# Layer 0's prologue with its token loads between the modulation halves and its norms ahead of the last halves

## The chip, the cores and the metric

The kernel runs on one core of one Trainium2 chip. The metric is device time in microseconds (us), the median of several runs; lower is better. A profiled execution also gives the time of every instruction on TensorE (PE, with its weight loads listed as PEld), VectorE (DVE), ScalarE (ACT), GpSimd (POOL) and the DMA issues of SyncE (SP). In the profile an engine name with a q behind it (SPq, ACTq) is that engine's queue.

## The reference, cut to what matters

The program is a two-layer diffusion backbone over 1024 latent tokens and 256 context tokens, model width 1024, in float32. Each layer begins in the same way: a conditioning vector gives a shift, a scale and a gate (the modulation), the tokens are RMS-normalised, scaled and shifted, and the result h feeds every projection of the layer.

```python
def rms_norm(x, g):
    y = xf * lax.rsqrt(jnp.mean(xf * xf, axis=-1, keepdims=True) + EPS)
    return (y * g.astype(jnp.float32)).astype(x.dtype)

def modulation(cond, w, b):
    m = jax.nn.silu(cond) @ w + b          # 1024 -> 3 * 1024
    return jnp.split(m, 3, axis=-1)        # shift, scale, gate

for i in range(DEPTH):                     # DEPTH = 2
    sh_l, sc_l, g_l = modulation(c, mod_w[i], mod_b[i])
    sh_c, sc_c, g_c = modulation(c_ctx, mod_w[i], mod_b[i])
    h_lat = rms_norm(x_lat, norm_g[i]) * (1.0 + sc_l[:, None, :]) + sh_l[:, None, :]
    h_ctx = rms_norm(x_ctx, norm_g[i]) * (1.0 + sc_c) + sh_c
    ...                                    # attention (layer 0), convolution and attention (layer 1)
    x_lat = x_lat + g_l[:, None, :] * y_lat
```

## The kernel before, in words

Activations lie with the model width on the partitions: 8 slices (dk) of 128 by the tokens. The tokens are cut in three chunks: chunk 0 is the 256 context tokens, chunks 1 and 2 are 512 latent tokens each. Products are made in split precision: every operand is kept as a high part and a low remainder, and one product is three matmuls (lines 316 to 318: high by high, high by low, low by high). So every h must be made as a pair, the high part by ACT and the low part by POOL or DVE.

The prologue of layer 0 is driven by a string, `PLAN`, one letter for one step, traced in this order:

- `p` loads the small bias and gain vectors.
- `0`, `1`, `2` ask for a chunk of tokens (tiles `xr`): chunk 0 as two DMAs, chunk 1 as two, chunk 2 as eight. All are issued from SP. `after_mod(XA)` puts a load behind the DMAs of the last four modulation tiles traced.
- `m` is one modulation half, `mod_half`: 512 output columns of shift or scale. Four weight tiles (`mw`, two dk slices each) come from HBM in a ring over buffers that the attention needs later (`KA`, `KB`, `V`) and two of its own; for each tile PE multiplies with the conditioning (`pm`, line 176, 32 columns of the array each); ACT copies the sum (`mrow`, line 203), eight small matmuls turn it round (`trm`, line 181), DVE adds the bias (`modT`, line 185), and for scale halves multiplies with the norm's gain (`gs`, line 187). The four halves are shift 0, shift 1, scale 0, scale 1; scale half 0 gives `gs` for dk 0 to 3, scale half 1 for dk 4 to 7.
- `n` is the sum of squares of the next chunk, `norm_x`: eight squares on ACT (lines 678 and 681) and seven additions on DVE (line 682) into `acc`.
- `b` is that chunk's reciprocal root laid over all partitions, `norm_bc`: matmuls with ones (`trs`, line 251), a power on POOL (line 238), three small DVE instructions (lines 239 to 241), and matmuls that broadcast the result (`bc`, line 261) into a PSUM bank.
- `w` asks for the first projection weights (`wr`), which ACT and POOL split (`wh`, `wl`). Two raw buffers serve four loads, so the last two wait until the first two are split.
- `h` makes the chunk's pair, `make_h`: for each dk one DVE multiplication by `gs` and `bc` (line 306), the shift on ACT (line 309 or 312), and the split (lines 296, 299, 310).

Behind the prologue `proj_qkv` makes ten blocks of 128 tokens, 24 matmuls each (`pq`): two blocks from chunk 0, four from chunk 1, four from chunk 2. Further modulation halves (the gate of layer 0 and all six of layer 1) are fed in between by `mod_steps`, with the same line 176.

The traced order is a priority and not yet the order of issue: the framework's scheduler fixes each engine's queue ahead of time on a simulated timeline (`schedule_with_timeline_sim=True`), taking what it believes ready. On the chip each queue then runs in that fixed order. PSUM banks are taken by tag: `st` has two banks, `ov` and `tr` one each; `trs` and `trm` share `tr`, `bc` uses `st`. `p0`, the pool of the projections' tiles, is opened when `st0`, the pool of the first two chunks' `xr`, is closed.

Of the kernel before, what the change touches and what calls it, by code (L numbers as in the profile page):

```python
# [69 lines left out]
HV = 'gggvvvvg'  # L70
O1 = (6, 65, 41, 14)
TICK0, TICK1 = (1, 3)
PLAN = 'p0mmnbwmm1h2nbhnbh'
MWR = "ABxAVx"
XA = 4
ORDER = (2, 3, 0, 1)
# [11 lines left out]
def tile_kernel(ctx: ExitStack, tc: tile.TileContext, a, out):  # L88
# [14 lines left out]
    def bank(tag, name):  # L103
        if tag == "pp" and solo[0]:
            turn[0] += 1
            tag = ("pp", "mx")[turn[0] // 2 % 2]
        return ps.tile([P, 512], F32, tag=tag, name=name, bufs=BUFS[tag])
# [3 lines left out]
    def nm(s):  # L111
        uid[0] += 1
        return f"{s}_{uid[0]}"
# [50 lines left out]
    @contextmanager  # L164
    def after_mod(k):

        with ExitStack() as cx:
            for m in mm0[-k:]:
                cx.enter_context(tc.issue_after(m.ins))
            yield  # L170
# [24 lines left out]
    def mod_half(l, part, j):  # L195

        pb = bank("pp", nm("pm"))
        for d2 in range(4):
            w2 = mw_tile()
            mm0.append(SY.dma_start(w2, mod_src(l, part, j, 2 * d2, 2 * d2 + 2)))  # L200
            mod_part(pb, w2, (2 * d2, 2 * d2 + 1))
        row = a0.tile([P, 512], F32, tag="ost", name=nm("mrow"), bufs=2)
        SC.copy(row, pb)
        mod_out(bank("tr", nm("trm")), row, l, part, j)
# [29 lines left out]
    def newton_rsqrt(pool, v, n, tag):  # L234

        r = pool.tile([P, 16], F32, tag=tag + "r", name=nm("nr"), bufs=2)
        t = pool.tile([P, 16], F32, tag=tag + "t", name=nm("nt"), bufs=2)
        GP.tensor_tensor(r[:, :n], v, mhalf[:, :n], op=ALU.pow)
        VE.tensor_tensor(t[:, :n], r[:, :n], v, op=ALU.mult)
        VE.scalar_tensor_tensor(t[:, :n], t[:, :n], -0.5, r[:, :n], op0=ALU.mult, op1=ALU.mult)  # L240
        VE.scalar_tensor_tensor(r[:, :n], t[:, :n], 1.5, r[:, :n], op0=ALU.add, op1=ALU.mult)
        return r

    def rstd_steps(pool, accs, n, tag, inv=1.0, tr="tr"):


        nb = n // P
        tr = bank(tr, nm("trs"))
        for b in range(nb):
            for k, acc in enumerate(accs):  # L250
                PE.matmul(tr[:, 2 * b : 2 * b + 2], acc[:, b * P : (b + 1) * P], ones, start=(k == 0),
                          stop=(k == len(accs) - 1))
        v = pool.tile([P, 8], F32, tag="rbv", name=nm("rbv"), bufs=2)
        VE.tensor_scalar(v[:, :nb], tr[:, 0 : 2 * nb].rearrange("p (b two) -> p b two", two=2)[:, :, 0],
                         inv, EPS, op0=ALU.mult, op1=ALU.add)
        r = newton_rsqrt(pool, v[:, :nb], nb, "rb")
        yield
        yield
        bc = bank(tag, nm("bc"))
        for b in range(nb):  # L260
            PE.matmul(bc[:, b * P : (b + 1) * P], r[:, b : b + 1].broadcast_to([P, P]), ident, start=True, stop=True)
        return bc
# [9 lines left out]
    def run(gen):  # L272

        while True:
            try:
                next(gen)
            except StopIteration as e:
                return e.value


    def new_h(c):
        if c == 0:
            t = bigp.tile([P, 2, DK, 256], F32R, tag="big", name=nm("hc"))
            return (t[:, 0], t[:, 1])
        th = bigp.tile([P, DK, 512], F32R, tag="big", name=nm("hh"))
        tl = bigp.tile([P, DK, 512], F32R, tag="big", name=nm("hl"))
        return (th, tl)
# [13 lines left out]
    def make_h(l, c, xs, bc, h):  # L301

        cond = 1 if c == 0 else 0
        for dk in range(DK):
            x = xs(dk)
            VE.scalar_tensor_tensor(x, x, gs[l][:, dk, cond : cond + 1], bc, op0=ALU.mult, op1=ALU.mult)
            shift = modT[l][:, dk, cond : cond + 1]
            if HV[dk] == "v":
                SC.activation(h[0][:, dk, :], x, AF.Identity, bias=shift)
                VE.scalar_tensor_tensor(h[1][:, dk, :], x, shift, h[0][:, dk, :].bitcast(F32), op0=ALU.add, op1=ALU.subtract)  # L310
            else:
                SC.activation(x, x, AF.Identity, bias=shift)
                split(x, h[0][:, dk, :], h[1][:, dk, :])
# [332 lines left out]
    with ExitStack() as p0x:  # L646
# [3 lines left out]
        def load_w0(src, u):  # L650
            return load_w(w0p, a[src], u, 384, W0B, rb=WRB)

        with tc.tile_pool(name="st0", bufs=1, reuse_waits="tile") as st0:
            for c in range(3):
                h[c] = new_h(c)
            xraw = {}

            def load_x(c):
                t0, n = CHUNKS[c]
                if c == 2:  # L660
                    tags = ["ph"] * 4 + ["pl"] * 4
                    xraw[c] = [a0.tile([P, n], F32, tag=t, name=nm("xr2"), bufs=LOOK0 + 1) for t in tags]
                else:
                    t = st0.tile([P, DK, n], F32, tag=f"xr{c}", name=f"xr{c}")
                    xraw[c] = [t[:, dk, :] for dk in range(DK)]
                    for d in range(0, DK, 4):
                        SY.dma_start(t[:, d : d + 4, :],
                                     a["cT"][:, d : d + 4, :] if c == 0 else a["xT"][:, d : d + 4, 0:n])
                    return
                for dk in range(DK):  # L670
                    SY.dma_start(xraw[c][dk], a["xT"][:, dk, t0 - 256 : t0 - 256 + n])

            def norm_x(c):
                n = CHUNKS[c][1]
                acc = kvp.tile([P, 512], F32, tag="QH", name=nm("acc"), bufs=3)
                for dk in range(DK):
                    if dk == 0:
                        SC.activation(acc[:, :n], xraw[c][0], AF.Square)
                    else:
                        sq = kvp.tile([P, 512], F32, tag="QL", name=nm("sq"), bufs=3)  # L680
                        SC.activation(sq[:, :n], xraw[c][dk], AF.Square)
                        VE.tensor_tensor(acc[:, :n], acc[:, :n], sq[:, :n], op=ALU.add)
                return acc

            def norm_bc(c, acc):
                n = CHUNKS[c][1]
                return run(rstd_steps(st0, [acc], n, "st"))[:, :n]

            made = [0]
            accs, bcs, mh = [], [], [(0, 0), (0, 1), (1, 0), (1, 1)]  # L690
            mwp[0] = st0
            for ev in PLAN:
                if ev in "012":
                    with after_mod(XA):
                        load_x(int(ev))
                elif ev == "p":
                    SC.dma_start(modb, a["mod_b"])
                    SC.dma_start(normg, a["norm_g"])
                elif ev == "n":
                    accs.append(norm_x(len(accs)))  # L700
                elif ev == "w":
                    with after_mod(XA):
                        w0 = load_w0("ev_qkv", ORDER[0])
                elif ev == "m":
                    mod_half(0, *mh.pop(0))
                elif ev == "b":
                    bcs.append(norm_bc(len(bcs), accs[len(bcs)]))
                elif ev == "h":
                    make_h(0, made[0], lambda dk, c=made[0]: xraw[c][dk], bcs[made[0]], h[made[0]])
                    made[0] += 1  # L710

            mwp[0] = None
# [142 lines left out]
        for k in range(4):  # L855
            u = ORDER[k]
            n = NSTEP[u // 2] + (12 if k == 0 else 0)
# [698 lines left out]
```

## Time and profile before

| what | value |
|---|---|
| median of 3 runs | 1595.98 us (1594.56 to 1597.62) |
| profiled execution, its time | 1590.1 us |
| its span, first to last instruction | 1588.3 us |
| PE busy | 1477.4 us, 93% of the span |
| DVE, POOL, ACT busy | 1087.8, 791.0, 745.3 us |
| HBM read and written | 153.84 and 54.79 MB |

Busy times are sums over an engine's instructions; the profile's windows give the same for a stretch, with the granted clock of TensorE (1.00 is full) and the DMA rate. A timeline row gives start, duration, engine, line and tile, and in brackets how long the engine had been idle and for what.

### The profile page before, as it was taken

How to read it: one execution, taken by the hardware profiler on the slowest of the kernel's cores; microseconds unless marked ns; L12 is line 12 of the kernel's file. 1: busy time of each engine (PE TensorE's matmuls, PEld its weight loads, DVE VectorE, ACT ScalarE, POOL GpSimd, SP SyncE). 2: the span in 40 equal slices, each digit the busy share in tenths (PEclk: the TensorE clock that was granted, in tenths of full speed). 3: DMA queues.
4: the chain of work that ended last, by engine and by line, in shares of the span. 5: the costliest groups of instructions: out<-in, count | busy, mean ns of one | idle time of the engine just before them, and what ended most of it. 6: DMA issues, size and time to landing. Idle time of an engine off the chain costs nothing.

```text
span 1588.3 us, 21721 instructions
## 1 busy us (share of the span) xinstructions
PE 1477.4 (93%) x7084; PEld 1178.0 (74%) x7084; DVE 1087.8 (68%) x2283; ACT 745.3 (47%) x1418; POOL 791.0 (50%) x633
## 2 busy tenths in 40 slices
PE   6899999999999999999989879999998899899995
PEld 2785988886886778876866657888877778777775
DVE  2833576588599855566778857999566465778776
ACT  3722334443435555457555754433333454545563
POOL 3531352553445676557555755654431343344575
PEclk7899999998999999999999989999999899899997
DMA  9473324422312363212112032213546877988732
GB/s 366 157 238 121 110 84 152 137 76 90 110 50 82 99 210 101 64 57 65 30 38 80 7 101 60 80 54 101 190 160 198 234 222 215 273 243 239 224 101 106
DMA packets 159929, 211.38 MB, mean 133 GB/s; under 512 B 15356, under 2 KB 96456, under 8 KB 159816
## 3 DMA queue, kind: packets, MB, share of 16 engines
q1 hardware_dynamic: 153152, 198.42, 39.8%
q10 hardware_dynamic: 6664, 11.57, 2.2%
q8 instruction: 56, 0.92, 0.3%
q14 instruction: 57, 0.47, 0.1%
HBM read 153.84 MB, written 54.79 MB: 131 GB/s over the span
## 4 chain that ended last, share of the span: by engine, by line
PE 67%; DVE 16%; DMA 7%; issue 4%; ACT 2%; POOL 2%; SPq 0%; DVEq 0%; ACTq 0%; POOLq 0%
PE p L316 6%; PE p L317 6%; PE p L318 6%; PE ov L426 4%; PE ov L428 4%; PE ov L427 4%; PE st L463 4%; PE st L467 3%; PE po L316 3%; PE po L317 3%; PE po L318 3%; PE pq L316 3%; PE pq L317 3%; PE pq L318 3%; PE pg L318 2%
## 5 line engine op out<-in xcount | busy, mean ns | idle before, releaser
L299 POOL TENSOR_TENSOR pl<-pf,ph 128x512 fp32r<-128x512 f32 (+4 forms) x321 | 393.8, 1238 | 361.5 <-ACT ph L296 289.4
L299 POOL TENSOR_TENSOR wl<-wr,wh 128x512 fp32r<-128x512 f32 (+2 forms) x131 | 170.6, 1314 | 181.1 <-ACT wh L296 150.6
L475 ACT ACTIVATE pf<-st 128x512 f32<-128x512 f32 x284 | 165.6, 596 | 200.7 <-PE st L467 153.0
L296 ACT CAST ph<-pf 128x512 fp32r<-128x512 f32 (+4 forms) x364 | 209.6, 588 | 27.9 <-PE ov L427 17.7
L316 PE MATMUL p<-hh,wh 128*128 128x512 f32 x448 | 180.1, 402 | 8.6 <-ACT hh L296 2.8
L317 PE MATMUL p<-hl,wh 128*128 128x512 f32 x448 | 178.7, 400 | 0.9 <-POOL hl L299 0.9
L318 PE MATMUL p<-hh,wl 128*128 128x512 f32 x448 | 176.4, 400 | 0.0
L463 PE MATMUL st<-QH,KAt 128*128 128x512 f32 (+4 forms) x364 | 142.6, 393 | 10.0 <-ACT pf L475 8.1
L426 PE MATMUL ov<-ph,Vt 128*128 128x512 f32 (+4 forms) x364 | 141.3, 388 | 7.8 <-DVE y L625 6.2
L428 PE MATMUL ov<-pl,Vt 128*128 128x512 f32 (+4 forms) x364 | 141.6, 389 | 1.6 <-POOL pl L299 0.9
L427 PE MATMUL ov<-ph,Vt 128*64 128x512 f32 (+4 forms) x364 | 139.8, 384 | 0.0
L467 PE MATMUL st<-QL,KBt 68*128 68x512 f32 (+4 forms) x364 | 136.6, 388 | 0.0
L1041 DVE SCALAR_TENSOR_TENSOR cps<-U,taps,cps 128x512 f32<-128x512 f32 x184 | 126.4, 751 | 0.9
L296 ACT CAST wh<-wr 128x512 fp32r<-128x512 f32 (+2 forms) x134 | 81.1, 613 | 88.8 <-PE p L317 19.9
L316 PEld LDWEIGHTS p<-hh,wh 128*128 128x128 f32 x448 | 85.5, 191 | 31.3 <-ACT hh L296 3.0
L588 DVE TENSOR_REDUCE mp<-mx 128x1 f32<-128x512 f32 x128 | 85.9, 683 | 28.1 <-PE mx L587 27.5
L317 PEld LDWEIGHTS p<-hl,wh 128*128 128x128 f32 x448 | 85.1, 190 | 21.8 <-POOL hl L299 1.9
L318 PEld LDWEIGHTS p<-hh,wl 128*128 128x128 f32 x448 | 85.1, 190 | 19.9
L316 PE MATMUL pq<-wh,hh 128*128 128x384 f32 x256 | 88.4, 345 | 2.8 <-ACT hh L296 2.8
L463 PEld LDWEIGHTS st<-QH,KAt 128*128 128x128 f32 x364 | 70.1, 193 | 28.1 <-ACT pf L475 12.1
L426 PEld LDWEIGHTS ov<-ph,Vt 128*128 128x128 f32 x364 | 70.5, 194 | 23.9 <-issue 6.9
L428 PEld LDWEIGHTS ov<-pl,Vt 128*128 128x128 f32 x364 | 70.2, 193 | 24.1 <-POOL pl L299 5.0
(274 smaller groups left out, 3508.4 us busy)
## 6 DMA issues: line engine op xcount, KB each, us to landing
mw<-in_mod_w_dram SPq DMA_DIRECT2D x16, 1024.0 KB, 6.1
Q<-qs SPq DMA_DIRECT2D x40, 256.0 KB, 2.1
QH<-Q SPq DMA_DIRECT2D x80, 128.0 KB, 2.7
mw<-in_mod_w_dram SPq DMA_DIRECT2D x16, 512.0 KB, 7.1
wr<-in_od_d_dram SPq DMA_DIRECT2D x32, 256.0 KB, 2.9
wr<-in_ev_qkv_dram SPq DMA_DIRECT2D x16, 384.0 KB, 5.0
KAt<-KD SPq DMA_DIRECT2D x16, 384.0 KB, 5.5
wr<-in_od_wo_dram SPq DMA_DIRECT2D x22, 256.0 KB, 3.8
```

What stands on the lines that cost most here:

```text
L296: SC.copy(hi, src)
L299: (GP if leng == "g" else VE).tensor_tensor(lo, src, hi.bitcast(F32), op=ALU.subtract)
L316: PE.matmul(o, lh, rh, start=first, stop=False)
L317: PE.matmul(o, lh, rl, start=False, stop=False)
L318: PE.matmul(o, ll, rh, start=False, stop=last)
L426: PE.matmul(o, V[:, 64:192], ph[:, :n], start=(t == 0), stop=False)
L427: PE.matmul(g.ov[0:64, q0 : q0 + n], V[:, 0:64], ph[:, :n], start=False, stop=False)
L428: PE.matmul(o, V[:, 64:192], pl[:, :n], start=False, stop=(last and g.sink is None))
L463: sts.append(PE.matmul(st[:, :n], KA[:, cs], g.QH[:, q0 : q0 + n], start=True, stop=False))
L467: PE.matmul(st[:, :n], KB[0:68, cs], g.QL[0:68, q0 : q0 + n], start=False, stop=True)
L475: SC.activation(pf[:, :n], st[:, :n], AF.Exp, scale=1.0 if g.bias else SCALE)
L1041: VE.scalar_tensor_tensor(pc, uc, w, pc, op0=ALU.mult, op1=ALU.add)
```

## The change

The order of the prologue's steps is another, and the third chunk's `bc` takes bank `ov` where it took `st`, since all three broadcasts are now traced before the first of them is used.

```diff
-PLAN = 'p0mmnbwmm1h2nbhnbh'
+PLAN = 'p0m1m2nwnmnmbbbhhh'
...
             def norm_bc(c, acc):
                 n = CHUNKS[c][1]
-                return run(rstd_steps(st0, [acc], n, "st"))[:, :n]
+                return run(rstd_steps(st0, [acc], n, ("st", "st", "ov")[c]))[:, :n]
```

Before, all four halves are traced ahead of the loads of chunks 1 and 2, the norm of chunk 0 stands between the shift and scale halves, and the norms of chunks 1 and 2 come between the making of one h and the next. After, chunk 1 is asked for behind the first half and chunk 2 behind the second; the norm of chunk 0 and the first projection weights come next; the norms of chunks 1 and 2 stand ahead of scale half 0 and scale half 1 in turn; the three broadcasts and then the three h are last.

## The prediction

> **What bounds the kernel now.** I read the page's span and slices first, then windows of the front of the span, then the timeline of the front.
>
> ```profile
> span 1588.3 us, 21721 instructions
> PE   6899999999999999999989879999998899899995
> 0.00:59.00 59.00, 38.40 (x176) 21.95 (x176) 24.40 (x65) 25.21 (x50) 16.65 (x21) 0.80 0.81 298
> 59.00:139.00 80.00, 79.09 (x424) 59.94 (x425) 38.69 (x75) 32.09 (x70) 33.26 (x25) 0.98 0.62 206
> ```
>
> TensorE is nearly full but for the first slice of the tenths and part of the second. The windows (length; busy time and count of PE, PEld, DVE, ACT, POOL; granted clock; DMA share; GB/s) put the border at 59 us: 38.40 busy before it, at clock 0.80, and 79.09 of 80 behind it. What the prologue loses until PE is full is therefore paid in the total, nearly one for one. The DMA engines bound the first part:
>
> ```profile
> 0.00:10.00 10.00, 1.11 (x4) 0.22 (x4) 3.52 (x14) 4.49 (x10) 0.99 (x7) 1.00 0.79 256
> 10.00:20.00 10.00, 7.58 (x36) 1.97 (x36) 0.63 (x3) 0.59 (x1) 0.00 (x0) 0.92 1.06 401
> 20.00:30.00 10.00, 8.12 (x40) 2.95 (x36) 0.81 (x5) 2.05 (x3) 4.84 (x4) 0.67 1.05 409
> 30.00:40.00 10.00, 9.27 (x39) 5.50 (x35) 4.04 (x9) 7.37 (x16) 7.45 (x7) 0.56 1.05 397
> ```
>
> That is 2.56, 6.57, 10.66 and 14.63 MB landed by 10, 20, 30 and 40 us. Then, on the timeline (start, duration, engine):
>
> ```profile
> 28.83 1.94 PE L176 MATMUL pm<-mw,csil 128*32 128x512 f32 x8
> 30.85 0.59 ACT L203 COPY mrow<-pm 128x512 f32<-128x512 f32 x1 [7.49 <-PE pm L176]
> 33.59 0.54 DVE L187 SCALAR_TENSOR_TENSOR gs<-modT,normg 128x8 f32<-128x8 f32 x1
> 36.84 0.69 PE L316 MATMUL pq<-wh,hc 128*128 128x384 f32 x1
> 39.59 0.95 PE L181 MATMUL trm<-msel,mrow 128*128 128x2 f32 x8
> 43.31 0.44 PE L316 MATMUL pq<-wh,hc 128*128 128x384 f32 x1 [0.24 <-ACT hc L309]
> 44.65 0.44 PE L318 MATMUL pq<-wh,hc 128*128 128x384 f32 x1 [0.38 <-DVE hc L310]
> 48.22 0.95 PE L251 MATMUL trs<-ones,acc 128*128 128x2 f32 x8
> 52.56 1.84 PE L251 MATMUL trs<-ones,acc 128*128 128x2 f32 x8 [3.39 <-DVE nt L240]
> 54.26 2.05 PE L261 MATMUL bc<-ident,nr 128*128 128x128 f32 x8
> 59.07 0.69 PE L316 MATMUL pq<-wh,hh 128*128 128x384 f32 x1 [2.76 <-ACT hh L296]
> 59.56 0.52 PE L317 MATMUL pq<-wl,hh 128*128 128x384 f32 x1
> 59.88 0.52 PE L316 MATMUL pq<-wh,hh 128*128 128x384 f32 x1
> 62.79 0.34 PE L316 MATMUL pq<-wh,hh 128*128 128x384 f32 x1
> 63.67 1.05 PE L261 MATMUL bc<-ident,nr 128*128 128x128 f32 x8
> 72.71 0.34 PE L316 MATMUL pq<-wh,hh 128*128 128x384 f32 x1
> 72.89 0.33 PE L317 MATMUL pq<-wl,hh 128*128 128x384 f32 x1
> 73.06 0.34 PE L318 MATMUL pq<-wh,hl 128*128 128x384 f32 x1
> 74.02 1.06 PE L176 MATMUL pm<-mw,csil 128*32 128x512 f32 x8
> ```
>
> The first projection matmul starts at 36.84 us. Chunk 0's 48 matmuls are through at 48.2; until 59.07 PE has nothing but norm matmuls, since chunk 1 is not normalised: its squares and sums ran late, between the steps of chunk 0's h. The idle stretch also drops the clock: successive pq start 0.32 us apart from 59.56, and 0.175 apart from 72.71 to 73.06.
>
> **The change, part by part.**
>
> *The moved loads.* No byte is added, and SP's queue order changes. Sizes:
>
> ```profile
> mw<-in_mod_w_dram SPq DMA_DIRECT2D x16, 512.0 KB, 7.1
> wr<-in_ev_qkv_dram SPq DMA_DIRECT2D x6, 384.0 KB, 5.3
> xr<-in_xT_dram SPq DMA_DIRECT2D x2, 1024.0 KB, 9.4
> xr<-in_xT_dram SPq DMA_DIRECT2D x8, 256.0 KB, 11.0
> xr<-in_cT_dram SPq DMA_DIRECT2D x2, 512.0 KB, 5.4
> ```
>
> So chunk 0 is 1.05 MB, a half 2.10, chunks 1 and 2 are 2.10 each, a weight load 0.39. Through scale half 0 the new order needs 1.05 + 3 × 2.10 + 2 × 2.10 + 2 × 0.39 = 12.3 MB; at the measured rates that lands at 30 + (12.3 − 10.66) / 0.397 = 34.2 us. Scale half 1 adds 2.10 and, if the other two weight loads pass it, 0.79: 15.2 MB, at 41.4 us (39.4 without them). The ten token DMAs go ahead of eight modulation DMAs on SP; the queue behind those is only as late as the bytes make it. Chunk 2 has landed at about 27 us (9.45 MB).
>
> *The first h.* Before, the last matmuls of scale half 0 end at 28.83 + 1.94 = 30.77 and the first pq starts 6.07 later: copy, turning, bias, gain, multiplication, shift, split. I take the same 6.07 after 34.2 plus 1.2 for the last tile's matmuls (half of the 1.94 for two tiles, and the landing's signal): first pq at 41.5, which is 4.7 us later than before. This is the price of the change.
>
> *The norms.* The same instructions at another place:
>
> ```profile
> L682 DVE TENSOR_TENSOR acc<-acc,sq 128x512 f32<-128x512 f32 x14 | 9.5, 687 | 1.6 <-ACT sq L681 1.2
> L681 ACT ACTIVATE sq<-xr 128x512 f32<-128x512 f32 x14 | 8.4, 627 | 1.7 <-DVE acc L682 1.7
> ```
>
> 9.5 us of DVE and 8.4 us of ACT leave the stretch between 37 and 52 us. From 10 to 30 us DVE is busy 1.44 and ACT 2.64 us by the windows above, so the new place has room; if chunk 2 came later than 27 us, its additions would fall back onto the first h.
>
> *The broadcasts.* Each chunk costs PE a trs (0.95) and a bc (1.05 at full clock), and a chain through POOL and DVE. Where they land the trace cannot show. Lower bound: all before 41.5, nothing. Upper: all six behind it, 3 × (0.95 + 1.05) = 6.0. PE waits for DMA until then, so I sit near the lower end with one trs and one bc, 2.0. Bank `ov` for the third costs nothing: in the solo stretch `mod_steps` also asks for `ov`, but its first matmuls come at 74.02, when chunk 2's h no longer holds it.
>
> *Chunk 0's second half.* From the end of scale half 0's pm to the end of its `gs` is 34.13 − 30.77 = 3.4 us, and from there to the first pq 2.7. With 0.7 for the last tile, scale half 1 gives `gs` near 45.5, and chunk 0's dk 4 near 48.2. Chunk 0's dk 0 to 3 are only 24 matmuls, 4.2 us and 1.8 more while the clock is half; the same dk of chunk 1 are 24 more, if the queues hold them there (the tags leave PSUM banks for four blocks). Bounds of the waiting: nothing, and 48.2 − (41.5 + 4.2) = 2.5. Before, the same place shows 0.24 + 0.38 = 0.62 of idle time (rows at 43.31 and 44.65). I take 1.2, about the middle.
>
> **The sum.** What PE loses from its first pq until it is full, beside the pq work itself (equal in both), with one more row for the first start:
>
> ```profile
> 38.29 0.52 PE L318 MATMUL pq<-wh,hc 128*128 128x384 f32 x1
> ```
>
> Before: half clock at the first start 1.0 (36.84 to 38.29 is four steps, 1.45 for 0.70, and two more like them), trm 0.95, idle 0.62, trs 0.95, the gap 59.07 − 49.17 = 9.9, half clock again 1.8 (59.07 to 62.79 is eleven steps, 3.72 for 1.93), bc 1.05: 16.3. After: later start 4.7, half clock once 1.8, the last tile's pm 1.0 and trm 0.95 in between, broadcasts 2.0, waiting 1.2: 11.7. Difference 4.6 us. PE behind it is 79.09 of 80, so I let it reach the end whole. Profiled 1590.1 − 4.6 = 1585.5; the profiled execution lies 5.9 below the median of the runs shown, so against 1595.98 the forecast is **1591.4 us**.
>
> **The rivals.** About 0.2%, 3.2 us, is what a measurement of this kernel tells from no change.
>
> *The norms do not get ahead (no change).* If the broadcasts stay behind scale half 1 in PE's queue, which is their traced place, or POOL's power waits behind a clearing of attention buffers, then after `gs` at about 45.5 come trs, the power and bc. POOL does wait like that now:
>
> ```profile
> 30.93 1.16 POOL L538 MEMSET KBt<- 4x1280 f32 x1 [3.38 <-DMA mw<-in_mod_w_dram]
> 54.67 1.01 POOL L238 TENSOR_TENSOR nr<-rbv,mhalf 128x4 f32<-128x4 f32 x1 [3.12 <-DVE rbv L254]
> ```
>
> One chain is at least 0.95 + 1.01 + 1.05 = 3.0 us (trs, power, bc) and at most the 6.0 from trs at 48.22 to bc at 54.26; I take 3.5 for the first chunk, which has half the blocks. First pq near 45.5 + 3.5 + 2.7 = 51.7: later start 14.9, half clock 1.8, one further trs and bc 2.0, 18.7 against 16.3, a loss of 2.4: 1598.4 us. A second warming, such as the gap before has behind it, would add 1.8 and make 1600.2, over the border; that end is counted with the slower case. Against this rival: pq runs at 36.84 ahead of the trm at 39.59, which is traced earlier, so the queues do take ready work first. The Trainium skill's page "TensorE: Matmul & The Clock Gate", in Part 1, says that an idle window of about 3.4 us halves the clock. By this rule only a wait of that length, and so not the 2.5 bounded above, brings the second warming; the trace agrees so far, with half clock after a gap of 9.9 and full clock after idle times of 0.24 and 0.38.
>
> *The layer 1 modulation falls apart (slower).* Eight more halves are fed between the projections, and their cost hangs on how the queue mixes them (the window is of line 176 alone):
>
> ```profile
> 105.31 1.92 PE L176 MATMUL pm<-mw,csil 128*32 128x512 f32 x16
> 120.00:130.00 10.00, 7.16 (x14) 1.00 0.56 182
> ```
>
> Sixteen in a row take 1.92 us; between 120 and 130 us fourteen strewn among other matmuls take 7.16, so a strewn half costs 16 × 0.51 − 1.92 = 6.3 us more. A front that moves by some us changes the scheduler's mixing. One more strewn half gives 1591.4 + 6.3 = 1597.7, no change; it decides from (4.6 + 3.2) / 6.3 = 1.2 halves; two give 1604.0 us. Against it: the halves are the same and are fed at the same steps. "TensorEngine Tiling" in the Trainium skill, under Key Properties, says that changing the tiling mode drains the array: a rule against any strewing, with which the 0.51 against 0.12 us each agrees.
>
> *They come together (more).* The same price the other way: one strewn half fewer, 1591.4 − 6.3 = 1585.1 us; the strewn stretch at 120 us is there to be gained.
>
> **How the numbers follow.** My forecast (3 to 8 us gained) 0.42; the halves packed better, or no waiting at all in the prologue, 0.15; norms not ahead, or one strewn half more, 0.25; two strewn halves or the like 0.18. So faster 0.57, same 0.25, slower 0.18. The range runs from 1584, the packed case with its own uncertainty, to 1602, where about half of the slower case is left out. The likeliest case alone spans 1588 to 1593.
>
> **What would show it.** Right: the first pq at 40 to 43 us; token DMAs of chunk 2 issued before 27 us; sums of squares over by 36; no PE gap above 3 us after the first pq; one stretch of half clock. Wrong: trs or bc of chunk 0 behind the last pm; a first pq above 46; line 176 behind 74 us in other groups than 8, 16 and the strewn stretch at 120; a PE gap that only moved to a later place.

## The result, and the profile after

The changed kernel takes 1599.28 us (median; 1595.42 to 1605.56), the kernel before 1595.86 us in the same series. The ratio is 1.0027, with a 95% interval of 1.0015 to 1.0039: slower by about 4 us, where 4.6 us of gain were forecast. The profiled execution of the changed kernel took 1596.89 us, its span is 1595.1.

First the slices of the span (PE's busy tenths), and the two windows of the front (length; busy time and count of PE, PEld, DVE, ACT, POOL; clock; DMA share; GB/s), to be held against those of before:

```profile
span 1595.1 us, 21718 instructions
PE   4899999998998999999989879999999899999995
0.00:59.00 59.00, 35.34 (x146) 18.80 (x147) 25.68 (x62) 23.44 (x46) 17.02 (x21) 0.71 0.79 288
59.00:139.00 80.00, 77.38 (x429) 59.74 (x427) 37.92 (x65) 32.51 (x68) 33.25 (x25) 1.00 0.59 190
```

By 59 us 146 matmuls have run where there were 176, and the window behind it is less full than before (77.38 against 79.09). PE's timeline shows why:

```profile
35.42 3.17 PE L176 MATMUL pm<-mw,csil 128*32 128x512 f32 x8 [0.75 <-DMA mw<-in_mod_w_dram]
41.07 3.64 PE L176 MATMUL pm<-mw,csil 128*32 128x512 f32 x16
45.42 1.87 PE L181 MATMUL trm<-msel,mrow 128*128 128x2 f32 x8 [0.71 <-ACT mrow L203]
47.54 1.01 PE L251 MATMUL trs<-ones,acc 128*128 128x2 f32 x4 [0.26 <-DVE modT L185]
48.81 1.87 PE L251 MATMUL trs<-ones,acc 128*128 128x2 f32 x8 [0.25 <-DVE rbv L254]
50.54 1.20 PE L261 MATMUL bc<-ident,nr 128*128 128x128 f32 x4
51.53 1.71 PE L251 MATMUL trs<-ones,acc 128*128 128x2 f32 x8
53.55 0.69 PE L316 MATMUL pq<-wh,hc 128*128 128x384 f32 x1 [0.31 <-ACT hc L296]
57.79 1.05 PE L261 MATMUL bc<-ident,nr 128*128 128x128 f32 x8
59.91 1.05 PE L261 MATMUL bc<-ident,nr 128*128 128x128 f32 x8
70.61 0.44 PE L318 MATMUL pq<-wh,hl 128*128 128x384 f32 x1 [1.49 <-DVE hl L310]
72.31 0.45 PE L318 MATMUL pq<-wh,hl 128*128 128x384 f32 x1 [0.38 <-DVE hl L310]
75.70 0.44 PE L318 MATMUL pq<-wh,hl 128*128 128x384 f32 x1 [0.37 <-DVE hl L310]
```

Chunk 0's norm matmuls (`trs` x4, at 47.54) stand behind the last matmuls (`pm`) and the last turning (`trm`) of scale half 1, and the `trs` of chunks 1 and 2 behind it. So the first projection starts at 53.55 us, 16.7 later than before. From there PE runs without the old gap of 9.9, but at about 70 us it waits for low parts of h, 2.6 us in four waits (the fourth, 0.39, is at 74.01). DVE's timeline names the cause of these:

```profile
58.88 10.62 DVE L306 SCALAR_TENSOR_TENSOR xr<-xr,gs,bc 128x512 f32<-128x512 f32 x16 [0.51 <-PE bc L261]
69.42 9.91 DVE L310 SCALAR_TENSOR_TENSOR hl<-xr,modT,hh 128x512 fp32r<-128x512 f32 x8
```

All sixteen multiplications of chunks 1 and 2 come first, and only then the low parts of chunk 1 that DVE makes.

To compare kernels beyond one row I use a *front mark*: the start of the 551st of the 7084 TensorE matmuls in the trace, at 128.7 us in the kernel before, where PE has been full for a long while in all of them. Up to there every kernel below has run the same matmuls, if in another order (240 `pq` and 124 `pm` among them). For the changed kernel the mark lies 5.0 us later. Further on the shift is larger, as the row of layer 1's first projection shows (count, shortest/median/longest ns, first and last start). Before it starts at 948.9:

```profile
L316 PE MATMUL p<-hh,wh x448: 389/396/794, 948.9 to 1366.8; 128*128 128x512 f32 x150
```

and in the changed kernel at 956.9, which is 8.0 later:

```profile
L316 PE MATMUL p<-hh,wh x448: 388/396/794, 956.9 to 1377.9; 128*128 128x512 f32 x150
```

Where the further 3.0 us between the mark and this row are lost was not traced. The medians differ by 3.4, so part of the 8.0 is regained in layer 1.

### The profile page after: what moved, and what is told of

Read it like the earlier page. It is cut to its first block, busy times and chain, and to the rows that moved or that the text cites. A ratio compares the mean times of both kernels' runs of the same rounds, so it can differ in the third digit from the quotient of the medians.

```text
span 1595.1 us, 21718 instructions
## 1 busy us (share of the span) xinstructions
PE 1474.8 (92%) x7084; PEld 1174.5 (74%) x7084; DVE 1092.8 (69%) x2283; ACT 748.1 (47%) x1418; POOL 792.3 (50%) x633
## 5 line engine op out<-in xcount | busy, mean ns | idle before, releaser
L318 PE MATMUL pq<-wh,hl 128*128 128x384 f32 x256 | 87.1, 341 | 2.6 <-DVE hl L310 2.6
```

What stands on the lines that cost most here:

```text
L318: PE.matmul(o, ll, rh, start=False, stop=last)
```

## The experiments

All ratios are to the kernel before, run on the same chip in the same series. The edits are given against the changed kernel. "Mark" is the shift of the front mark against the kernel before, read in each kernel's profiled execution.

| kernel | median us | before us | ratio, 95% interval | first pq us | mark us |
|---|---|---|---|---|---|
| changed kernel | 1599.28 | 1595.86 | 1.0027 (1.0015 to 1.0039) | 53.55 | +5.0 |
| e3 loads only | 1602.02 | 1594.79 | 1.0050 (1.0030 to 1.0071) | 45.98 | +6.0 |
| e4 norms only | 1582.21 | 1594.79 | 0.9926 (0.9906 to 0.9947) | 43.98 | -2.1 |
| c1, e4 once more | 1583.50 | 1595.21 | 0.9929 (0.9914 to 0.9944) | 44.04 | -2.3 |
| e8 one load | 1597.55 | 1595.01 | 1.0007 (0.9989 to 1.0026) | 51.06 | +2.9 |
| e1 broadcasts ahead | 1592.65 | 1594.79 | 0.9987 (0.9969 to 1.0004) | 46.94 | -1.1 |
| e2 `trs` in own bank | 1595.78 | 1594.79 | 1.0009 (0.9994 to 1.0024) | 47.20 | +2.8 |
| e9 e4 with own bank | 1595.43 | 1595.01 | 1.0004 (0.9989 to 1.0018) | 32.36 | -0.5 |
| e5 h of chunk 2 late | 1598.97 | 1595.01 | 1.0032 (1.0018 to 1.0047) | 52.90 | +4.6 |
| e13 two `bc` in `ov` | 1586.71 | 1595.21 | 0.9952 (0.9934 to 0.9970) | 53.44 | +2.7 |
| e14 e1 with two `bc` in `ov` | 1593.62 | 1595.21 | 0.9996 (0.9982 to 1.0011) | 48.52 | +1.7 |
| e15 chunk 1 first | 1589.95 | 1595.21 | 0.9966 (0.9951 to 0.9981) | 46.92 | -2.6 |
| e10 front of before | 1596.24 | 1593.96 | 1.0007 (0.9990 to 1.0024) | 34.92 | +1.6 |
| e17 own bank, two `bc` in `ov` | 1586.79 | 1593.96 | 0.9952 (0.9936 to 0.9968) | 44.73 | -7.2 |

**Which half of the change costs?** One kernel moves the loads alone, one the norms alone, one the norms and one load.

```diff
-PLAN = 'p0m1m2nwnmnmbbbhhh'
+PLAN = 'p0m1m2nbwmmhnbhnbh'     # e3, with all three bc in st
+PLAN = 'p0mmnwmm12nnbbbhhh'     # e4
+PLAN = 'p0m1mnwmm2nnbbbhhh'     # e8
```

> The load part of the change alone: tokens asked for between the modulation halves, all other steps in the order of before (plan p0m1m2nbwmmhnbhnbh, all broadcasts in st). Theory Q: the first pq near 45 us as in the other experiments, 8 us later than before, and a gap behind chunk 0 that is some 4 us shorter, since the squares are early but the broadcast of chunk 1 still waits behind the last trm; total within 3 us of before (ratio 0.999 to 1.003). Theory B: all of the change's loss is here, ratio 1.002 to 1.004.

> The norm part alone: loads of chunks 1 and 2 behind all four halves as before, all norms and broadcasts ahead of the three h (plan p0mmnwmm12nnbbbhhh, third broadcast in ov). Theory Q: broadcast of chunk 0 behind the last trm near 40 us, first pq near 45, then a gap until chunk 1 is normalised near 56; total 2 to 6 us above before (ratio 1.001 to 1.004). Theory B: no loss without the moved loads, ratio 0.999 to 1.001.

> The norms-first plan with only chunk 1's tokens moved, in between shift halves, and chunk 2 asked for behind all halves (plan p0m1mnwmm2nnbbbhhh): 2.1 MB ahead of the scale halves, where the norms-only kernel has none and the changed kernel 4.2. Front marker: the time of the 551st TensorE matmul, 128.7 us before; 5.0 later in the changed kernel, 2.1 earlier in norms-only. Theory B (bytes ahead of the scale halves set the start): first pq near 48 to 50 us (norms-only 44.0, changed 53.6), marker 1 to 2 us later than before. Theory Q (the queue position of the broadcasts alone): first pq as in the changed kernel and marker 4 to 5 later.

At the mark the loads alone cost 6.0 us and the norms alone gain 2.1; together 3.9, against 5.0 for both at once. With one load moved it is +2.9, between them, though later than the 1 to 2 that I expected. So in these kernels the loss goes with the bytes put ahead of the scale halves. But the first pq tells more: loads alone delay it by 9.1 us, norms alone by 7.1, both together by 16.7. Something other than bytes delays it by 7.6 beyond the loads alone. (e4's total gains far more than its mark, which neither theory had; see below.)

**Is it the broadcasts' place in PE's queue?** e1 traces two of them ahead of the scale halves; e2 keeps the plan and lets `trs` take bank `ov`, so that it does not share `tr` with `trm`.

```diff
+PLAN = 'p0m1m2nbwnbmnbmhhh'     # e1
...
-                return run(rstd_steps(st0, [acc], n, ("st", "st", "ov")[c]))[:, :n]
+                return run(rstd_steps(st0, [acc], n, ("st", "st", "ov")[c], tr="ov"))[:, :n]   # e2
```

> The changed kernel with each chunk's broadcast step traced right behind its norm (plan p0m1m2nbwnbmnbmhhh), so that all three stand ahead of scale half 1. Theory Q (queue: the broadcasts stood behind scale half 1 in TensorE's queue, first pq at 53.6 us instead of some 45): first pq at 44 to 47 us, the total 5 to 8 us under the changed kernel, that is 0 to 4 us under before (ratio 0.997 to 1.000). Theory B (bytes: the tokens ahead of the scale halves cost all of it): the first pq comes earlier, but the time stays within 2 us of the changed kernel (ratio about 1.002). Theory S (scatter of the later schedule, the front does not matter): total unrelated to the first pq, within 3 us of the changed kernel.

> The changed kernel with its plan as it is, but the sums trs taken in PSUM tag ov and not in tr, which the modulation's trm use. Theory Q says that the single bank of tr, handed out in traced order, is what held trs behind the last trm: with another tag the broadcasts run ahead although they are traced last; first pq at 44 to 47 us, ratio to before 0.997 to 1.000. If instead traced order as such holds them back, first pq stays near 53 us and the ratio near 1.002. Theory S: no relation.

Yes. e1's first pq comes 6.6 us earlier than the changed kernel's and its mark 6.1; the two intervals do not touch. In e2 the trace order is the changed kernel's, only the bank differs, and the first pq comes 6.4 earlier. That it gains only 2.2 at the mark has a second cause, in PE's timeline of e2:

```profile
34.63 1.84 PE L251 MATMUL trs<-ones,acc 128*128 128x2 f32 x8 [4.77 <-DVE acc L682]
39.92 1.16 PE L261 MATMUL bc<-ident,nr 128*128 128x128 f32 x8
42.85 1.05 PE L181 MATMUL trm<-msel,mrow 128*128 128x2 f32 x8
```

Now all three `trs` are ahead, and the last waits for chunk 2's sums while the scale halves stand behind it: scale half 0 is turned at 42.85 (39.27 in the changed kernel). What is late next is again set by the queue.

**Do DVE's multiplications of chunk 2 hold up chunk 1?** e5 traces chunk 2's broadcast behind the first two h; e13 puts the broadcasts of chunks 1 and 2 both in `ov`, which is one bank, so that the third cannot be made before chunk 1 is done with the second.

```diff
+PLAN = 'p0m1m2nwnmnmbbhhbh'     # e5
...
+                return run(rstd_steps(st0, [acc], n, ("st", "ov", "ov")[c]))[:, :n]   # e13; e14 with e1's plan
```

> The changed kernel with the broadcast of chunk 2 traced behind the h of chunk 1 (plan p0m1m2nwnmnmbbhhbh). Theory D (with all three h together VectorE runs the sixteen multiplications of chunks 1 and 2 ahead of the low parts of chunk 1, and TensorE waits 3 us for them between 69 and 76 us): those waits for hl on line 310 shrink under 1 us, and the marker is 1 to 3 us later than before and not 5.0. If the waits are the rate of VectorE and not its order, they stay or move, and the marker is 4 to 6 later.

> The changed kernel, plan as it is, with the broadcasts of chunks 1 and 2 both in the single bank ov, so that chunk 2's multiplications cannot run before chunk 1's are through. Theory D (VectorE's order: sixteen multiplications ahead of chunk 1's low parts cost TensorE 3.2 us between 69 and 76 us): the waits for hl fall under 1 us, the marker (551st TensorE matmul, 5.0 later than before in the changed kernel) is 1.5 to 3 later. Theory rate (VectorE has too much to do there in any order): marker 4 to 6.

> The same two banks on top of the plan with the broadcasts ahead (p0m1m2nbwnbmnbmhhh), whose marker is 1.1 us earlier than before, with one wait of 2.3 us for a low part at 68 us. Theory D: that wait goes, marker 2.5 to 4 earlier. Theory rate: marker stays at 1 earlier. Total by the marker 1590 to 1594 us, by scatter of the later schedule 4 us either way.

e5 says nothing of this: chunk 2's `bc` was still issued at 59.59, and the waits were nearly the same. By line and tile its TensorE and DVE instructions stand in the very order of the changed kernel, so it is that kernel once more: first pq 0.65 earlier, mark 0.3 lower, layer 1's first projection at 957.0 (956.9). e13 does: first pq, clock and the first `trs` are those of the changed kernel, but DVE's rows now alternate,

```profile
58.79 5.36 DVE L306 SCALAR_TENSOR_TENSOR xr<-xr,gs,bc 128x512 f32<-128x512 f32 x8 [0.51 <-PE bc L261]
64.06 4.85 DVE L310 SCALAR_TENSOR_TENSOR hl<-xr,modT,hh 128x512 fp32r<-128x512 f32 x4
68.83 5.34 DVE L306 SCALAR_TENSOR_TENSOR xr<-xr,gs,bc 128x512 f32<-128x512 f32 x8
```

PE has no wait from 53.75 to 85 us, and the mark goes from +5.0 to +2.7: 2.3 us, against 2.6 of waits counted. That e13's total is 12.6 below the changed kernel's is another matter (below). e14 was a miss: e1's wait of 2.30 for a low part is gone, but its mark is worse than e1's by 2.8, since its first pq is 1.6 later and a `pq` of chunk 0 waits 1.78 at 57.88 for ACT. So that DVE's order costs something is shown in e13 alone.

**Is the first pq what counts?**

```diff
+PLAN = 'p0mmnwmm12nnbbbhhh'     # e9: e4's plan, with tr="ov"
+PLAN = 'p0m1mnbwnbmm2hhnbh'     # e15
```

> Norms-only (loads behind all halves, as before) with trs in PSUM tag ov, so that the broadcasts need not wait for the last trm. Theory B with Q: neither cost is left; first pq at 36 to 39 us as before, chunk 1 ready some microseconds sooner than before's 59.1, marker 3 to 6 us earlier than before, total ratio 0.995 to 0.998 if the later part of the schedule stays alike. Theory S (the later schedule decides): ratio anywhere between 0.992 and 1.004 whatever the marker.

> A plan from the theories B, Q and D together: chunk 1 alone asked for between the shift halves, chunk 2 behind all halves, broadcasts of chunks 0 and 1 ahead of the scale halves, chunk 2's norm and h behind the others (p0m1mnbwnbmm2hhnbh). If bytes, queue place and VectorE's order are the causes, first pq at 40 to 44 us, no gap of over 2 us behind it, marker 4 to 8 us earlier than before. If the front is bound by something else, marker within 2 us of before.

No, not alone. e9 starts it at 32.36, 4.5 before the kernel before, and its mark moves by 0.5, where 3 to 6 were expected: chunk 1's h comes at 58.66 in both (59.07 before). In e4 the first pq is 7.1 later than before and the mark 2.1 better. Its chunk 1 comes at 59.27 and no sooner, but chunk 0's matmuls now reach close to it and the clock is not lost. What counts in these kernels is from when on PE is full without a break. e15, with chunk 1 alone moved and both first chunks broadcast ahead, gets -2.6, short of the 4 to 8 expected: its first pq comes at 46.92, not at 40 to 44.

**The totals do not follow the marks: e4 and e13.** Their fronts differ by 4.8 us, and yet both end some 10 us below what their marks say. Two repeats without any edit:

> The kernel before once more, for its scatter from one execution to the next. If the shifts in the front are the program's, the times of the matmuls of layer 0 (to about 949 us) agree with the first profile of before within 1 us; what differs by more in layer 1 is the chip's scatter and not an effect of a plan. Theory S in its strong form (each program's later order sets the rest): layer 1 agrees within 1 us as well.

> The norms-only kernel once more (p0mmnwmm12nnbbbhhh), which was 12 us faster in the total with a marker only 2.1 earlier. If its later schedule is better as a program, the ratio is 0.990 to 0.995 again and layer 1 takes some 8 us less than before's in this profile too. If the first timing was a favourable draw, the ratio comes to 0.997 to 1.000.

e4's gain repeats (0.9929). The kernel before, once more (1594.56, one execution), has its mark within 0.2, though its first pq is 1.1 earlier, and is 4.4 us later near the end (6951st matmul): one program scatters by that in layer 1. The first profile of the kernel before lies 5.9 below its median, so it is a low one to hold others against there.

Comparing the order of TensorE's matmuls by line and tile, the last three quarters of e4 and e13 are one and the same order, matmul for matmul. In the last 15% there are three orders in all: A (before, e14), B (changed kernel, e1, e2, e5, e8, e9, e15; e3 but for a few places), C (e4, e13). The edits of the front decide which of them the scheduler falls into. So a theory: the total is the mark plus a constant of the order. Two kernels try it: e10 has nearly the front of before, with order B; e17 has the changed kernel's plan, `trs` in `ov`, the last two `bc` in `ov`, with order A.

```diff
+PLAN = 'p0mmnbwmm12nnbbhhh'     # e10
...
+                return run(rstd_steps(st0, [acc], n, ("st", "ov", "ov")[c], tr="ov"))[:, :n]   # e17
```

> Plan p0mmnbwmm12nnbbhhh: the loads stand as in the kernel before, only the third broadcast goes to the other PSUM bank. Its TensorE order in the front is nearly that of the kernel before, but its order in the last third is the one that the changed kernel has (order B), not that of the kernel before (order A). Theory O (the time is the front's shift plus a constant of the late order: A 0, B about -1, C about -10 us): front shift about -1 to +1, so 1593 to 1596, ratio 0.998 to 1.000. Rival F (the late gain of 8 to 10 us in the norms-only kernel follows from the norms being ahead in the front, which this plan has nearly as much): 1584 to 1587, ratio below 0.995. Rival N (order B is worse than A by itself and is what made the changed kernel slower): 1598 or more.

> The changed kernel's plan, its norms' turning matmuls in the other bank and the last two broadcasts there as well. The late order is that of the kernel before (order A), while the kernel with its own bank but only the third broadcast there has order B (median 1595.78, front shift +2.8). Theory O: front shift +2 to +4, no late gain, so 1596 to 1599, ratio 1.001 to 1.003. Rival F (whatever follows the front follows it in layer 1 too, the order does not matter): as the kernel with the banks shared and the last two broadcasts in the other (front +2.7, 1586.71), so 1587, ratio 0.995.

e10: 1596.24, mark +1.6 (a little over the -1 to +1 expected), so B's constant is +0.7 here; a late gain that follows from the norms would have given 1584, and it is not there. e17's total (1586.79) is the number that the rival had, but its place is not the rival's: the mark is -7.2, the total -7.2, and nothing is gained late. My forecast of its front (+2 to +4) was the miss. Median minus that of before minus mark, for all: order A -3.3 (e14) and 0.0 (e17); order B -1.6, -1.0, -1.8, +1.2, -0.6, -0.4, +0.9, -2.7, +0.7; order C -10.5, -9.4 and -11.2. C's gain is not there yet when layer 1's first projection starts (948.9 before). In e13 that is 949.9:

```profile
L316 PE MATMUL p<-hh,wh x448: 389/396/794, 949.9 to 1370.0; 128*128 128x512 f32 x150
```

e17's gain is there, with 941.9:

```profile
L316 PE MATMUL p<-hh,wh x448: 389/396/794, 941.9 to 1363.0; 128*128 128x512 f32 x150
```

From the 5351st matmul (about 1191 us) to the 6951st, e4, its repeat and e13 gain 7.7, 7.7 and 6.9 us; the changed kernel gains 0.9. Against the repeat of the kernel before, the gain would be 4.7 larger. What in order C is better was not found, and that the order is the cause is not shown: it was never changed by itself. For this change it suffices that the changed kernel has order B, whose constant is small in nine kernels (+1.2 to -2.7): its loss is the front's, to within some 3 us.

**e17: the same plan with other banks.** PE's timeline:

```profile
23.21 1.02 PE L251 MATMUL trs<-ones,acc 128*128 128x2 f32 x8 [0.89 <-DVE acc L682]
26.26 1.13 PE L261 MATMUL bc<-ident,nr 128*128 128x128 f32 x8 [0.54 <-DVE nr L241]
39.39 1.05 PE L181 MATMUL trm<-msel,mrow 128*128 128x2 f32 x8 [0.69 <-ACT mrow L203]
42.87 1.94 PE L176 MATMUL pm<-mw,csil 128*32 128x512 f32 x8 [1.43 <-DMA mw<-in_mod_w_dram]
56.01 0.95 PE L251 MATMUL trs<-ones,acc 128*128 128x2 f32 x8
62.97 1.05 PE L261 MATMUL bc<-ident,nr 128*128 128x128 f32 x8
```

the windows of its front:

```profile
0.00:59.00 59.00, 39.02 (x197) 22.96 (x198) 32.91 (x70) 30.56 (x58) 22.03 (x24) 0.86 0.80 294
59.00:139.00 80.00, 79.17 (x440) 60.45 (x439) 34.71 (x79) 28.50 (x64) 29.08 (x23) 1.00 0.65 219
```

and DVE's first multiplications:

```profile
41.17 4.29 DVE L306 SCALAR_TENSOR_TENSOR xr<-xr,gs,bc 128x256 f32<-128x256 f32 x8
```

Chunk 0's `trs` runs at 10.74, chunk 1's broadcast is through at 27 us; as soon as scale half 0 is there, DVE multiplies dk 0 to 3 of both chunks, so chunk 1's matmuls (from 50.46) fill PE while scale half 1's h is made (its first high parts are used at 52.19, its low parts from 56.81). Only chunk 1's `bc` has another bank than in e2, yet the mark is 10.0 better: chunk 2's `trs`, which held PE 4.77 us in e2, stands at 56.01 here and its `bc` at 62.97, and no wait follows. From 44.73 to 85 us PE waits for nothing, with 197 matmuls done by 59 us. The same loads, the same plan, a mark 12.1 us ahead of the changed kernel's and a median 12.5 lower: the bytes put ahead cost 7.9 us of start (44.73 against 36.84), and are no loss where nothing breaks PE's run behind it. e4, with order C, is the fastest of all (1582.21 and 1583.50), below both kernels; e17's front with order C was not tried.

## Why the prediction was wrong

The step that failed is *the broadcasts*. I put them at 2.0 of at most 6.0 us, near the lower end, because PE would be waiting for DMA and "the queues do take ready work first". All three `trs` stood behind the last `trm`. A bound that counts PE's own time for them (three times 2.0) misses what matters: behind scale half 1 they hold up the first h, and for that delay the sum had nothing. The 2.0 as such is close to the two `bc` behind the first pq (2.1). From scale half 0's last `pm` (38.59) to the first pq it is 14.96 us where I took 6.07: 8.9 over. Two of the four signs that I had named for being wrong are there: `trs` of chunk 0 behind the last `pm`, and a first pq above 46. The evidence that I used, pq running ahead of an earlier traced `trm`, was from two tiles in different banks; `trs` and `trm` share the one bank of `tr`, which is handed out in traced order, and giving `trs` another bank moved them ahead (e2, e17). The rival "the norms do not get ahead" had the place and the mechanism, with first pq at 51.7 (measured 53.55) and 1598.4 us (1599.28); it had 0.25, shared with one strewn half more, and not the larger share. That its time comes so near is in part luck: its sum has no wait for low parts (2.6), its start is 1.8 too early, and the total is 1.5 below what the mark says.

*The moved loads* were too cheap by 3.2 us. Scale half 0's matmuls ended at 38.59, not at 34.2 + 1.2 = 35.4. DMA moved 407 GB/s between 30 and 40 us, as fast as assumed; but in SP's queue one tile of scale half 1 stands ahead of the last of scale half 0, and its 0.52 MB are 1.3 us of it. The last tile's weights went into PE at 36.66:

```profile
36.66 0.19 PEld L176 LDWEIGHTS pm<-mw,csil 128*32 128x32 f32 x4 [1.05 <-DMA mw<-in_mod_w_dram]
```

From there to 38.59 it is 1.9 us where I took 1.2, which is 0.7 more. The remaining 1.2 of the landing I did not trace. Token DMAs before 27 us (the last issued by 24.8) and sums of squares by 36 (34.2) came as forecast.

*The first h* at 41.5 was out of reach for these reasons: even with the broadcasts ahead it is 44.73 (e17) to 46.94 (e1). The 6.07 itself came near in e17, where the first pq is 6.03 behind scale half 0's last `pm` (38.70); but there PE stands 1.43 us waiting for a tile of scale half 1 just ahead of it, so this is in part chance.

*Chunk 0's second half* (1.2 of waiting) did not wait at all, since everything was late. In its place stand 2.6 us of waits for low parts behind DVE's sixteen multiplications, which I had not named; without them e13's mark is 2.3 better.

*The norms* were right: 9.5 us of DVE and 8.4 of ACT moved ahead, PE waited for none of it, and the gap of 9.9 did go. *The sum*: the loss after was to be 11.7 against 16.3. By the same ledger the changed kernel loses 16.7 of later start, 1.5 at half clock, 2.1 for two `bc` and 2.6 of waits: 22.9, which is 6.6 more than before, where the mark says 5.0. e17 loses 7.9 of later start, 0.6 at half clock, 0.95 for `trm`, 0.95 for `trs`, 1.05 for `bc`: 11.5. That this is nearly the forecast 11.7 is luck, since the start is 3.2 over and the half clock, the `pm` and the waiting are under. There the ledger gives -4.8 and the mark -7.2, so it holds to some 2 us.

*That the front goes through to the end whole* holds within an order to some 4 us (A: 0.0 and -3.3, B: +1.2 to -2.7), which is nearly the size of the gain that was forecast, and not on the way there: the changed kernel's +5.0 is +8.0 at layer 1's first projection and +3.4 in the median. It was also not known that an edit of the front can change the order of layer 1, with which some 10 us went in e4 and e13. The rival on layer 1's modulation is out: line 176 is busy 44.74 us over the whole span before and 43.83 after, and the strewn stretch from 120 to 150 us has 16 matmuls in 8.36 us before and in the changed kernel (line 176 alone; PE, PEld, clock, DMA share, GB/s):

```profile
120.00:150.00 30.00, 8.37 (x16) 1.10 (x16) 1.00 0.65 217
```

The page "Perfetto Trace Analysis" of the Trainium skill, in Optimizing Tensor Performance under Matmuls, says that independent groups of matmuls should rotate through different PSUM banks. The trace agrees in the outcome, first pq at 53.55 with the shared bank and at 47.20 with another; but its reason, that the emptying of one bank overlaps the next group, is not what acted here: `trs` was held by the order in which the bank is handed out.

## What to carry to other kernels

Before counting on early work running early, ask what it shares with late work: one PSUM bank taken in traced order puts a ready norm behind a matmul that waits for DMA, and moving every piece ahead gains little where one of them has to wait for its own data (e2). Judge an early matmul by whether the rest can follow without a break, not by its start. Where a scheduler fixes the queues, measure an edit by its own stretch as well as by the total, since an unrelated stretch may be laid out anew and be worth more than the edit.

## What the runs showed of the hardware that was not expected

Small matmuls can keep PE busy and the clock down. In the changed kernel PE is busy 8.78 of the 10 us from 40 to 50, with turning matmuls, norm sums and 32-column ones, at a granted clock of 0.50:

```profile
40.00:50.00 10.00, 8.78 (x40) 5.54 (x39) 3.36 (x10) 2.25 (x3) 6.02 (x5) 0.50 0.54 175
```

The Trainium skill's page "TensorE: Matmul & The Clock Gate", Part 1, says that about 3.4 us of sustained activity bring the full clock; the ten microseconds of the row, busy to 0.88, did not do so here, and full pace (pq starting 0.17 us apart and no longer 0.32) came only 3.0 us after the first pq. So a stretch of that length in which PE counts as busy is not enough by itself. Whether it is the kind of matmul or the idle time between them that matters was not tried.
